# Down projection: accumulating transfers issued four pairs ahead, token sums split before the sums that wait

## The chip, the cores and the metric

The kernel runs on one core of a Trainium2 chip. The metric is device time in microseconds (us) of one execution. The time before is the median of three runs. Engines: TensorE (PE, with its weight loads PEld), VectorE (DVE), ScalarE (ACT), GpSimd (POOL), SyncE (SP); 16 DMA engines move data between HBM and the on-chip buffers.

## What is computed

One layer of a hybrid encoder on 256 tokens of width 2048, in float32: a half-step SwiGLU feed-forward network (FFN), a mixer (a gated recurrence beside windowed attention), and a second FFN, each between RMS norms. The change touches the two FFNs' last matrix product alone, the down projection:

```python
def swiglu(x, w_gate_up, w_down):
    gate, up = jnp.split(x @ w_gate_up, 2, axis=-1)
    return (jax.nn.silu(gate) * up) @ w_down

ff = swiglu(rms_norm(x, pre_norm_ffn1[layer]), w_ffn1_gate_up[layer], w_ffn1_down[layer])
x = x + 0.5 * rms_norm(ff, post_norm_ffn1[layer])
```

`w_down` has 5632 rows and 2048 columns in float32 (46 MB in each of the two FFNs), and is read from HBM once.

## The kernel before

**Products.** A float32 operand is split into a high part `h` (a cast on ScalarE, L176) and a low part `l` (the source minus `h`, on VectorE, L177). A product is three matmuls: high x high, high x low, low x high (`three`, L435; the matmul is L441). The 256 tokens are two halves of 128 (m), the columns of a run two halves of 512 (n).

**Pairs, runs and steps.** The 5632 rows are 22 pairs of 256 (two blocks of 128, k). The projection is done in two runs of 1024 columns, each over all 22 pairs in the order of `orders` (L1197). A step is one pair of one run: steps 0 to 21 are run 0, 22 to 43 run 1; the last two pairs of run 1 (20, 21) are held for `finish` (L705). The silu-gated activations of a pair lie in a tile `ht`. Eight of the `ht` tiles (pairs 0 to 7) are put away to HBM earlier and fetched into four buffers (`fetch`, L1063, at the steps of `fetch_at`).

**Two kinds of pair.** A plain pair (odd numbers, 20 and 21) is 2 x 2 x 2 products, 24 matmuls, and its weights are split in two halves of 128x1024 (`split_half`, L168). A pair by sums (even numbers 0 to 18, `MIXED`) uses a scheme with seven products in place of eight, 21 matmuls (`products`, L485). It needs sums of weight blocks and sums of token blocks (the token sums). With b11, b12, b21, b22 the four 128x512 blocks of the raw weights, its steps are, in `splits` (L1238): split b11 alone (`ha`, `la`); form two block sums (L1255, one VectorE operation on 128x1024), or let a DMA do it; split the lower half; b22 = b11 + b22 (L1259); b21 = b22 + b21 (L1260); split the upper half; split the lower half again (the last half). The token sums, formed once when the activations were made, are split into `sp` (`left_sums`, L635). The order of use on TensorE: three matmuls with `ha`/`la`; three with the lower half; from the seventh on `sp` is needed; from the tenth the upper half; from the sixteenth the last half.

**Accumulating transfers.** For the pairs in `added` (L1202) the two block sums of L1255 are made by a DMA: `prepare(i)` (L1228) splits b11 into `ha`, `la` and then issues, on POOL's queue, a transfer of 512 KB that adds b12 and b22, read again from HBM, onto the first two blocks of the raw buffer (L1232). POOL waits for `la`, since the transfer overwrites b11. L1259 is the first operation on VectorE that reads the result.

**Order.** The loop at L1318 is under a schedule written by hand: what is written first is issued first on each engine. Iteration i does: first part of `splits(i + 1)`; `prepare(i + 3)`; fetches; second part of `splits(i + 1)`; the matmuls of step i; the last part of `splits(i + 1)`. In a pair by sums the parts end after L1260, after the upper half, and after the last half and `sp`.

**Loads.** Five raw buffers of 1 MB are in turn: three that last the whole kernel and two in the pool `hb`. When the last half of a pair has been split, its buffer takes the next load in the order `coming` (`load_down`, L1211), on SP's queue. `in_order` (L1204) sorts the steps, with those in `added` 2.5 places early. Loads from step 39 on (`NU + 17`) go to the lasting buffers only, since the pool `hb` is closed at step 40.

**Kept sums.** Run 0's splits of the token sums of pairs 0 and 2 (`near`) and 16 and 18 (`keep`) are kept for run 1; the others are split again. The unsplit sums of 16 and 18 are made during run 0 (`sums_again`, L1026, tile `su`).

**Fold.** After a run's last pair by sums, its four extra banks `p` are added to the four result banks `c` (`fold`, L513): in run 0 within step 20, in run 1 at step 41, ahead of that step's matmuls. After run 0 `second_run` (L698) drains the four banks `c` with ScalarE (squares) and VectorE (gains).

Of the kernel before, what the change touches and what calls it, by code (L numbers as in the profile page):

```python
# [12 lines left out]
F32R = mybir.dt.float32r  # L13
# [7 lines left out]
P = 128  # L21
# [16 lines left out]
def hymba_layer_kernel(  # L38
# [37 lines left out]
    def nm(s):  # L76
        uid[0] += 1
        return f"{s}_{uid[0]}"
# [89 lines left out]
    def split_half(raw, i, hp=hip, lp=lop):  # L168
        part = raw[:, i * 1024 : (i + 1) * 1024]
        h = hp.tile([P, 1024], F32R, tag="h", name=nm("h"))  # L170
        l = lp.tile([P, 1024], F32R, tag="l", name=nm("l"))
        split_act(h, l, part)
        return h, l

    def split_act(hi, lo, src):
        nc.scalar.copy(hi, src)  # L176
        nc.vector.tensor_tensor(lo, src, hi.bitcast(F32), ALU.subtract)  # L177
# [11 lines left out]
    far = {}  # L189
# [142 lines left out]
    class LeadN:  # L332


        def __init__(self, w, c0, slot):
            self.w, self.c0, self.slot = w, c0, slot
# [259 lines left out]
    class Pairs(Blocks):  # L596
# [2 lines left out]


        HELD = 2

        def __init__(self, w, orders, tiles, sums, room, gain_src, keep=(), near=()):

# [45 lines left out]

        def one_block(self):
            return (
                far["pool"].tile([P, 512], F32R, tag=t, name=nm(t)) for t in ("ha", "la")
            )

        def half_gain(self, pool):
# [48 lines left out]
        def finish(self, mul, post, new_x=None, gain=None, lead=None):  # L705
# [4 lines left out]
            self.post = post  # L710
            self.work(n_order - self.HELD)
            held = []
            for u in order[n_order - self.HELD :]:
                held.append((u, *split_load(self.source(u), hp=post, lp=post)))
# [150 lines left out]
    NU = DFF // 256  # L865
# [5 lines left out]
    MIXED = range(0, 20, 2)  # L871
# [133 lines left out]
    def ffn(gated, w_dn, post_gain, again, gain=None, lead=None, aside=None):  # L1005

        with ExitStack() as st:
            work = st.enter_context(tc.tile_pool(name=nm("wk"), bufs=1, reuse_waits="tile"))
# [5 lines left out]
            hts, sums, away = [], {}, {}  # L1014
# [165 lines left out]
            def pair_ahead(g, u):  # L1180
# [16 lines left out]
            orders = [  # L1197
                [9, 11, 8, 13, 10, 15, 12, 1, 0, 3, 14, 5, 16, 17, 2, 7, 4, 19, 6, 18, 20, 21],

                [7, 2, 9, 4, 11, 6, 13, 8, 10, 15, 0, 5, 12, 3, 14, 1, 16, 18, 17, 19, 20, 21],  # L1200
            ]
            added = {0: (12, 0, 14, 16, 2, 4, 6), 1: (2, 4, 6, 8, 0, 12, 14, 16)}  # L1202
            steps = [(r, u) for r in range(2) for u in orders[r]][: 2 * NU - Pairs.HELD]
            in_order = sorted(  # L1204
                (i - 2.5 if u in added[r] else i, i) for i, (r, u) in enumerate(steps)
            )
            coming = [i for _, i in in_order]
            raws, firsts, got = {}, {}, {}
            rows = None

            def load_down(raw):  # L1211
                if coming and (coming[0] < NU + 17 or any(raw is one for one in gated.lasting)):
                    i = coming.pop(0)
                    r, u = steps[i]
                    dst = raw.rearrange("p (k c) -> p k c", k=2)
                    nc.sync.dma_start(dst, Pairs.part(w_dn, u, r))
                    raws[i] = raw
# [10 lines left out]
            def prepare(i):  # L1228
                if i < len(steps) and steps[i][1] in added[steps[i][0]]:
                    r, u = steps[i]  # L1230
                    first_block(i)
                    nc.gpsimd.dma_start(  # L1232
                        raws[i][:, 0:1024].rearrange("p (k c) -> p k c", k=2),
                        Pairs.part(w_dn, u, r)[:, :, 512:1024],
                        accum_op=ALU.add,
                    )

            def splits(i):  # L1238
                if i >= len(steps):
                    return  # L1240
                r, u = steps[i]
                raw = raws[i]
                parts = got[i] = []
                b11, b12, b21, b22 = blocks(raw)
                if u not in MIXED:
                    parts.append(split_half(raw, 0))
                    yield
                    parts.append(split_half(raw, 1))
                    load_down(raw)
                    yield  # L1250
                    return
                four = raw.rearrange("p (i c) -> p i c", i=4)
                if i not in firsts:
                    first_block(i)
                    nc.vector.tensor_tensor(  # L1255
                        four[:, 0:2], four[:, 0::3], four[:, 1:2].to_broadcast([P, 2, 512]), ALU.add
                    )
                parts.append(split_half(raw, 1))
                nc.vector.tensor_tensor(b22, b11, b22, ALU.add)  # L1259
                nc.vector.tensor_tensor(b21, b22, b21, ALU.add)  # L1260
                yield
                parts.append(split_half(raw, 0))
                yield
                parts.append(split_half(raw, 1))
                load_down(raw)
                rows.left_sums_ahead(u)
                yield

            def products(i, among=None):
# [11 lines left out]
            with tc.manual_schedule():  # L1281
                gated.prepare(1, MIXED_IN[0])
                some(gated.splits(1, 0), 2)
                for g in range(1, NG):
                    first_pairs(g, waiting)
                    for u in range(2, last - 1):
                        pair_ahead(g, u)
                    some(gated.splits(g, last), 2)
                    if g < NG - 1:
                        gated.prepare(g + 1, MIXED_IN[0])  # L1290
                    for one in gated.take(g, last - 1):
                        one()
                    boundary(g, gated.splits(g + 1, 0) if g < NG - 1 else splits(0))
                    waiting = units(gated.c, rest)
                    some(waiting, 2)
                room_cm.__exit__(None, None, None)
                close_far()
                back_cm = tc.tile_pool(name=nm("hb"), bufs=AWAY // 2, reuse_waits="tile")
                back = back_cm.__enter__()
                fetch_at = {2: (1, 0), 3: (3,), 5: (5,), 9: (2,), 10: (7,), 11: (4,), 13: (6,)}  # L1300
                fetch_at.update({26: (0, 5), 28: (3,), 30: (1,)})
                again_at = {8: 16, 14: 18}
                for u in MIXED[8:]:
                    sums[u] = None
                rows = Pairs(w_dn, orders, hts, sums, work, post_gain, keep=MIXED[8:], near=MIXED[:2])
                some(waiting, 2)
                ahead = splits(1)
                some(ahead, 2)
                products(0)
                for _ in range(2):  # L1310
                    load_down(back.tile([P, 2048], F32, tag="raw", name=nm("raw"), bufs=2))
                some(waiting, 1)
                ahead = splits(2)
                some(ahead, 2)
                some(waiting, 1)
                some(ahead, 1)
                products(1)
                for i in range(2, len(steps)):  # L1318
                    if i == NU + 18:
                        back_cm.__exit__(None, None, None)  # L1320
                        early_cm.__exit__(None, None, None)
                        post = rows.post = st.enter_context(post_pool())
                    ahead = splits(i + 1)
                    next(ahead, None)
                    prepare(i + 3)
                    for u in fetch_at.get(i, ()):
                        fetch(u)
                    next(ahead, None)
                    products(i)
                    for _ in ahead:  # L1330
                        pass
                    if i in again_at:
                        sums[again_at[i]] = sums_again(again_at[i])
                    if i == 8:
                        rows.half_gain(far["pool"])
                    if i == NU - 1:
                        rows.second_run()
# [8 lines left out]
    gated = Gated(w_ffn1_gate_up[0], two_banks())  # L1346
    xt = new_xt()
    gated.see(xt)
    with tc.manual_schedule():
# [9 lines left out]
        raw = rawp.tile([P, 2048], F32, tag="raw", name=nm("raw"))  # L1359
# [121 lines left out]
    with ExitStack() as s2:  # L1481
# [111 lines left out]
        keep = [mid.tile([P, 2, 2, P], F32, tag=f"keep{j}", name=f"keep{j}") for j in range(2)]  # L1593
# [286 lines left out]
        orders = [[0, 1, 4, 6, 5, 7, 2, 3], [0, 4, 1, 5, 6, 7, 2, 3]]  # L1880
        rows = Pairs(w_mix_out[0], orders, yt, ysums, yroom, post_norm_mix)
# [3 lines left out]
        gated = Gated(w_ffn2_gate_up[0], two_banks())  # L1885
# [80 lines left out]
```

## Time and profile before

| | us |
|---|---|
| median of 3 runs | 1848.81 |
| lowest and highest | 1846.79, 1853.28 |
| the profiled execution | 1848.27 |
| its span, first to last instruction | 1846.4 |
| mean granted TensorE clock | 0.997 |

In that execution the down projection's steps 0 to 41 run from 477.62 to 705.20 us in the first FFN and from 1602.10 to 1826.69 us in the second; the text calls the two FFNs layers where it counts per layer. The rows below come from the page of the profile (busy time of engines, groups of instructions), from its views of busy time by stretch, of waits, of DMA issues, and from the timeline. A group's row has: line, engine, operation, out<-in, shape, count | busy us, mean ns of one | idle us of the engine just before them and who ended it. `L177 DVE` is an instruction of line 177 on VectorE; `pa` and `pb` are the result banks.

### The profile page before, as it was taken

Reading aid. Unit: us, or ns where it says so; the run is one execution under the profiler, and the core shown is the slowest. Engines: PE = TensorE matmul, PEld = TensorE weight load, DVE = VectorE, ACT = ScalarE, POOL = GpSimd, SP = SyncE. Lnnn points to the kernel's source line nnn. Section 1 sums busy time; section 2 is a strip of 40 time slices with the busy share of each in tenths; the row PEclk is TensorE's granted clock in tenths of the full one; section 3 lists DMA queues with packets and bytes.
Section 4 is the critical chain, followed back from the end, with each engine's and each line's share of the span. In section 5 each row is a group of like instructions: output and inputs, shape, how many; then the busy total and the mean of one; then the engine's idle time right before and its main releaser. Section 6 shows DMA issues by size and latency. Waiting matters only on the chain.

```text
span 1846.4 us, 23441 instructions
## 1 busy us (share of the span) xinstructions
PE 1819.5 (99%) x8438; PEld 1504.8 (82%) x8438; DVE 1601.5 (87%) x2041; ACT 1128.7 (61%) x1492; POOL 150.7 (8%) x145
## 2 busy tenths in 40 slices
PE   9999999999999999999999999999999999999997
PEld 6888888888877787888888888788888888878876
DVE  7999999999889888477687798899999999989886
ACT  6566666655556556476587557556666665556563
POOL 1011111111010100000000000011111111010110
PEclk9999999999999999999999999999999999999999
DMA  8789999989697885656554456789989989698874
GB/s 299 228 237 282 277 279 253 257 251 253 242 310 242 248 275 187 207 176 179 171 171 148 162 210 247 227 236 271 283 265 275 250 250 252 214 310 283 267 241 166
DMA packets 209332, 442.35 MB, mean 240 GB/s; under 512 B 11592, under 2 KB 46496, under 8 KB 208448
## 3 DMA queue, kind: packets, MB, share of 16 engines
q1 hardware_dynamic: 180032, 385.14, 59.5%
q0 software_dynamic: 29184, 55.72, 17.8%
q8 instruction: 66, 1.08, 0.2%
q14 instruction: 50, 0.41, 0.1%
HBM read 428.21 MB, written 12.60 MB: 239 GB/s over the span
## 4 chain that ended last, share of the span: by engine, by line
PE 71%; DMA 9%; issue 9%; DVE 8%; ACT 3%; POOL 1%; SPq 0%; DVEq 0%; ACTq 0%; POOLq 0%
PE pa L441 29%; PE pb L441 25%; DMA raw<-in_w_ffn_down_dram 6%; PE pa L309 5%; DVE l L177 3%; PE pa L314 3%; DMA raw<-in_w_ffn_gate_up_dram 2%; PE pa L364 2%; PE pa L363 2%; PE pa L362 2%; ACT h L176 1%; DVE raw L1259 1%; DVE la L177 1%; POOL raw L1232 0%; PE pa L1098 0%
## 5 line engine op out<-in xcount | busy, mean ns | idle before, releaser
L176 ACT CAST h<-raw 128x1024 fp32r<-128x1024 f32 (+1 forms) x861 | 851.1, 1013 | 484.6 <-PE pb L441 154.7
L177 DVE TENSOR_TENSOR l<-raw,h 128x1024 fp32r<-128x1024 f32 (+1 forms) x861 | 981.2, 1171 | 122.1 <-ACT h L176 90.2
L441 PE MATMUL pa<-h,xt 128*128 128x512 f32 x1104 | 387.6, 392 | 0.1
L441 PE MATMUL pb<-h,xt 128*128 128x512 f32 x952 | 340.7, 392 | 0.4 <-DVE pb L1150 0.4
L441 PEld LDWEIGHTS pa<-h,xt 128*128 128x128 f32 x1104 | 207.2, 188 | 44.2 <-DVE xt L232 0.6
L441 PE MATMUL pa<-l,xt 128*128 128x512 f32 x552 | 215.5, 390 | 0.0
L441 PEld LDWEIGHTS pb<-h,xt 128*128 128x128 f32 x952 | 178.7, 188 | 43.8 <-DVE pb L1157 3.9
L441 PE MATMUL pb<-l,xt 128*128 128x512 f32 x476 | 185.6, 390 | 0.0
L441 PE MATMUL pa<-h,ht 128*128 128x512 f32 x464 | 163.2, 390 | 2.6 <-DVE pa L535 2.6
L441 PE MATMUL pb<-h,ht 128*128 128x512 f32 x464 | 163.2, 390 | 0.0
L934 POOL DMA_DIRECT2D raw<-in_w_ffn_gate_up_dram x76 | 92.0, 1211 | 737.7 <-DVE l L177 654.6
L309 PE MATMUL pa<-xt,h 128*128 128x512 f32 x512 | 124.4, 393 | 0.2 <-ACT h L176 0.2
L441 PEld LDWEIGHTS pa<-l,xt 128*128 128x128 f32 x552 | 103.8, 188 | 20.6 <-DVE l L177 0.5
L309 PEld LDWEIGHTS pa<-xt,h 128*128 128x128 f32 x512 | 93.8, 188 | 18.6 <-ACT h L176 0.6
L441 PE MATMUL pa<-h,xs 128*128 128x512 f32 x304 | 108.9, 389 | 0.0
L441 PE MATMUL pb<-h,xs 128*128 128x512 f32 x304 | 106.0, 389 | 0.0
L441 PEld LDWEIGHTS pa<-h,ht 128*128 128x128 f32 x464 | 87.1, 188 | 21.6 <-issue 2.3
L441 PEld LDWEIGHTS pb<-l,xt 128*128 128x128 f32 x476 | 89.4, 188 | 17.0
L441 PEld LDWEIGHTS pb<-h,ht 128*128 128x128 f32 x464 | 87.4, 188 | 18.2
L441 PE MATMUL pb<-l,ht 128*128 128x512 f32 x232 | 90.5, 390 | 0.0
L441 PE MATMUL pa<-l,ht 128*128 128x512 f32 x232 | 90.3, 389 | 0.0
L441 PE MATMUL pa<-h,sp 128*128 128x512 f32 x176 | 63.8, 404 | 10.1 <-DVE sp L177 6.7
(287 smaller groups left out, 2529.7 us busy)
## 6 DMA issues: line engine op xcount, KB each, us to landing
raw<-in_w_ffn_gate_up_dram SPq DMA_DIRECT2D x350, 512.0 KB, 5.9
raw<-in_w_ffn_down_dram SPq DMA_DIRECT2D x88, 1024.0 KB, 7.5
raw<-in_w_mix_in_dram SPq DMA_DIRECT2D x52, 1024.0 KB, 4.9
raw<-in_w_ffn_gate_up_dram POOLq DMA_DIRECT2D x76, 512.0 KB, 8.7
raw<-in_w_mix_out_dram SPq DMA_DIRECT2D x16, 1024.0 KB, 5.1
raw<-in_w_ffn_down_dram POOLq DMA_DIRECT2D x30, 512.0 KB, 6.3
ht<-away SPq DMA_DIRECT2D x24, 512.0 KB, 9.4
away<-ht SPq DMA_DIRECT2D x16, 512.0 KB, 7.0
```

The costliest lines, as they stand in the source:

```text
L176: nc.scalar.copy(hi, src)
L177: nc.vector.tensor_tensor(lo, src, hi.bitcast(F32), ALU.subtract)
L309: nc.tensor.matmul(slot[f], weights(hs, kk, f), xcol(xt, k), start=(k == 0), stop=(k == KT - 1))
L314: nc.tensor.matmul(slot[f][:, 0:T], weights(ls, kk, f), xcol(xt, kh * 8 + kk, 0), start=False, stop=False,)
L362: nc.tensor.matmul(dst, xh, h[:, o : o + n], start=(k == 0), stop=False)
L363: nc.tensor.matmul(dst, xh, l[:, o : o + n], start=False, stop=False)
L364: nc.tensor.matmul(dst, xl, h[:, o : o + n], start=False, stop=(k == KT - 1))
L441: nc.tensor.matmul(self.bank(at), lhs, rhs, start=(n == 1), stop=n in (ends, self.of[at]), skip_group_check=n > ends,)
L934: nc.gpsimd.dma_start(raw[:, 0:1024].rearrange("p (k c) -> p k c", k=2), self.source(u, g)[:, :, 1], accum_op=ALU.add,)
L1259: nc.vector.tensor_tensor(b22, b11, b22, ALU.add)
```

## The change

It issues the accumulating transfers one step earlier (`prepare(i + 4)`) and moves the loads of their pairs one place ahead in the order of loads (3.5 places instead of 2.5); gives the FFNs' `ha` and `la` three buffers each instead of two; splits the token sums right after a pair's first half, ahead of L1259, instead of at the end; adds pair 18 to the accumulating ones in run 0, and 10 and 18 in place of 8 in run 1 (8 and 9 instead of 7 and 8); gives run 1 another order, which begins with pair 2; no longer keeps the splits of 16 and 18; lets loads of steps 39 and 40 go to any buffer; and shifts some fetches by a step.

```diff
--- before.py
+++ after.py
@@ -599,6 +599,7 @@
 
 
         HELD = 2
+        firsts = 2
 
         def __init__(self, w, orders, tiles, sums, room, gain_src, keep=(), near=()):
 
@@ -650,7 +651,8 @@
 
         def one_block(self):
             return (
-                far["pool"].tile([P, 512], F32R, tag=t, name=nm(t)) for t in ("ha", "la")
+                far["pool"].tile([P, 512], F32R, tag=t, name=nm(t), bufs=self.firsts)
+                for t in ("ha", "la")
             )
 
         def half_gain(self, pool):
@@ -1197,19 +1199,19 @@
             orders = [
                 [9, 11, 8, 13, 10, 15, 12, 1, 0, 3, 14, 5, 16, 17, 2, 7, 4, 19, 6, 18, 20, 21],
 
-                [7, 2, 9, 4, 11, 6, 13, 8, 10, 15, 0, 5, 12, 3, 14, 1, 16, 18, 17, 19, 20, 21],
+                [2, 7, 4, 9, 6, 11, 8, 13, 10, 12, 15, 0, 5, 14, 3, 16, 1, 18, 17, 19, 20, 21],
             ]
-            added = {0: (12, 0, 14, 16, 2, 4, 6), 1: (2, 4, 6, 8, 0, 12, 14, 16)}
+            added = {0: (12, 0, 14, 16, 2, 4, 6, 18), 1: (2, 4, 6, 10, 12, 0, 14, 16, 18)}
             steps = [(r, u) for r in range(2) for u in orders[r]][: 2 * NU - Pairs.HELD]
             in_order = sorted(
-                (i - 2.5 if u in added[r] else i, i) for i, (r, u) in enumerate(steps)
+                (i - 3.5 if u in added[r] else i, i) for i, (r, u) in enumerate(steps)
             )
             coming = [i for _, i in in_order]
             raws, firsts, got = {}, {}, {}
             rows = None
 
             def load_down(raw):
-                if coming and (coming[0] < NU + 17 or any(raw is one for one in gated.lasting)):
+                if coming and (coming[0] < NU + 19 or any(raw is one for one in gated.lasting)):
                     i = coming.pop(0)
                     r, u = steps[i]
                     dst = raw.rearrange("p (k c) -> p k c", k=2)
@@ -1256,6 +1258,7 @@
                         four[:, 0:2], four[:, 0::3], four[:, 1:2].to_broadcast([P, 2, 512]), ALU.add
                     )
                 parts.append(split_half(raw, 1))
+                rows.left_sums_ahead(u)
                 nc.vector.tensor_tensor(b22, b11, b22, ALU.add)
                 nc.vector.tensor_tensor(b21, b22, b21, ALU.add)
                 yield
@@ -1263,7 +1266,6 @@
                 yield
                 parts.append(split_half(raw, 1))
                 load_down(raw)
-                rows.left_sums_ahead(u)
                 yield
 
             def products(i, among=None):
@@ -1297,12 +1299,13 @@
                 close_far()
                 back_cm = tc.tile_pool(name=nm("hb"), bufs=AWAY // 2, reuse_waits="tile")
                 back = back_cm.__enter__()
-                fetch_at = {2: (1, 0), 3: (3,), 5: (5,), 9: (2,), 10: (7,), 11: (4,), 13: (6,)}
-                fetch_at.update({26: (0, 5), 28: (3,), 30: (1,)})
+                fetch_at = {2: (1,), 3: (0,), 5: (3,), 6: (5,), 9: (2,), 10: (7,), 11: (4,), 13: (6,)}
+                fetch_at.update({25: (0,), 26: (5,), 28: (3,), 29: (1,)})
                 again_at = {8: 16, 14: 18}
                 for u in MIXED[8:]:
                     sums[u] = None
-                rows = Pairs(w_dn, orders, hts, sums, work, post_gain, keep=MIXED[8:], near=MIXED[:2])
+                rows = Pairs(w_dn, orders, hts, sums, work, post_gain, near=MIXED[:2])
+                rows.firsts = 3
                 some(waiting, 2)
                 ahead = splits(1)
                 some(ahead, 2)
@@ -1322,7 +1325,7 @@
                         post = rows.post = st.enter_context(post_pool())
                     ahead = splits(i + 1)
                     next(ahead, None)
-                    prepare(i + 3)
+                    prepare(i + 4)
                     for u in fetch_at.get(i, ()):
                         fetch(u)
                     next(ahead, None)
```

## Prediction

> **What bounds the kernel now.** The page first: TensorE is hardly ever idle, so only a place where it waits, or runs slowly, can give time back.
>
> ```profile
> span 1846.4 us, 23441 instructions
> PE 1819.5 (99%) x8438; PEld 1504.8 (82%) x8438; DVE 1601.5 (87%) x2041; ACT 1128.7 (61%) x1492; POOL 150.7 (8%) x145
> ```
>
> A busy PE is not one at its peak, so the second view is the busy time by stretch, cut at the steps of the two down projections (columns: PE, PEld, DVE, ACT, POOL busy with counts, granted clock, DMA share, GB/s; the two rows with one count are of L441's matmuls alone).
>
> ```profile
> 477.62:596.08 118.46, 115.09 (x508) 93.89 (x506) 105.42 (x124) 68.52 (x84) 9.71 (x8) 1.00 0.88 289
> 596.08:652.40 56.32, 53.45 (x226) 43.18 (x225) 47.66 (x52) 33.24 (x39) 6.05 (x5) 0.97 0.82 262
> 1602.10:1718.47 116.37, 114.94 (x507) 93.92 (x506) 105.18 (x124) 68.62 (x84) 9.68 (x8) 1.00 0.90 294
> 1718.47:1774.39 55.92, 53.52 (x227) 43.16 (x225) 47.57 (x52) 33.23 (x39) 6.05 (x5) 0.97 0.83 265
> 1640.78:1676.82 36.04, 36.04 (x161) 29.85 (x160) 31.48 (x39) 22.09 (x25) 4.84 (x4) 1.00 1.01 338
> 692.52:705.20 12.68, 11.15 (x49) 1.00 0.72 257
> 1814.51:1826.69 12.18, 11.16 (x50) 1.00 0.23 88
> ```
>
> The fifth row is steps 7 to 13 of the second FFN: by the code 3 x 21 + 4 x 24 = 159 matmuls (two of the 161 only reach in) without a wait, so one takes 36.04 / 159 = 0.2267 us when nothing is late. A run has 10 x 21 + 12 x 24 = 498 of them, 112.9 us. Rows 1 and 3 (run 0) also hold eight transposes, which take 0.79 us:
>
> ```profile
> 1607.54 0.27 PE L1098 MATMUL pa<-ident,z 128*128 128x128 f32 x1
> 1608.33 0.48 PE L441 MATMUL pa<-h,ht 128*128 128x512 f32 x1
> ```
>
> Run 0 thus loses 118.46 - 112.9 - 0.8 = 4.8 us in the first FFN and 116.37 - 113.7 = 2.7 us in the second. Rows 2 and 4 are steps 22 to 31, 5 x 21 + 5 x 24 = 225 matmuls, 51.0 us: 5.3 and 4.9 us are lost. Together **17.7 us**. Part of it is clock: 0.97 in those rows, 0.03 x 56 = 1.7 us each.
>
> Third, who is waited for (the waits of 477 to 690, then of 1600 to 1812; total, times, longest):
>
> ```profile
> PEld pa L441 <- DVE sp L177: 5.9, 5, 1.5
> PEld pa L441 <- ACT sp L176: 3.3, 2, 1.9
> DVE raw L1259 <- DMA raw<-in_w_ffn_down_dram: 15.2, 9, 4.9
> ...
> PEld pa L441 <- DVE sp L177: 5.0, 5, 1.5
> PEld pa L441 <- ACT sp L176: 1.7, 2, 1.2
> DVE raw L1259 <- DMA raw<-in_w_ffn_down_dram: 15.6, 10, 4.1
> ```
>
> TensorE waits only for `sp`, the split token sums, and VectorE, which makes them, sits 15 us per layer before L1259, for the accumulating transfer to land. The timeline of VectorE at step 6 shows the one making the other:
>
> ```profile
> 1626.12 2.55 DVE L177 TENSOR_TENSOR l<-raw,h 128x1024 fp32r<-128x1024 f32 x2
> 1632.75 0.69 DVE L1259 TENSOR_TENSOR raw<-raw 128x512 f32<-128x512 f32 x1 [4.08 <-DMA raw<-in_w_ffn_down_dram]
> 1633.48 0.69 DVE L1260 TENSOR_TENSOR raw<-raw 128x512 f32<-128x512 f32 x1
> 1634.09 0.68 DVE L177 TENSOR_TENSOR la<-raw,ha 128x512 fp32r<-128x512 f32 x1
> 1634.69 2.35 DVE L177 TENSOR_TENSOR l<-raw,h 128x1024 fp32r<-128x1024 f32 x2
> 1636.96 0.68 DVE L177 TENSOR_TENSOR sp<-sums,sp 128x512 fp32r<-128x512 f32 x1
> ...
> 1762.46 0.19 PEld L441 LDWEIGHTS pa<-h,sp 128*128 128x128 f32 x1 [1.20 <-ACT sp L176]
> 1764.26 0.30 PEld L441 LDWEIGHTS pa<-h,sp 128*128 128x128 f32 x2 [1.50 <-DVE sp L177]
> ```
>
> 4.08 us idle, and `sp` is the last of six operations behind it. `la` of step 8 is queued there as well, so the next accumulating transfer is issued late too. The last two rows are step 30 (10 right behind 8), the costliest place.
>
> **The change part by part.** Unit prices, from the groups of 1600 to 1718 and from the instructions on the tile `su` (last row):
>
> ```profile
> L177 DVE TENSOR_TENSOR l<-raw,h 128x1024 fp32r<-128x1024 f32 x56 | 66.4, 1219 | 1.0 <-ACT h L176 0.8
> L177 DVE TENSOR_TENSOR la<-raw,ha 128x512 fp32r<-128x512 f32 x11 | 7.5, 686 | 0.0
> L1260 DVE TENSOR_TENSOR raw<-raw 128x512 f32<-128x512 f32 x10 | 6.9, 692 | 0.3
> L1255 DVE TENSOR_TENSOR raw<-raw 128x1024 f32<-128x1024 f32 x3 | 3.7, 1225 | 0.1
> L176 ACT CAST sp<-su x4: 614/614/617, 540.8 to 1702.4; 128x512 fp32r<-128x512 f32 x4
> L177 DVE TENSOR_TENSOR sp<-su,sp x4: 683/684/687, 542.5 to 1703.7; 128x512 fp32r<-128x512 f32 x4
> ```
>
> *Four pairs ahead.* An accumulating transfer is issued one step earlier, 4.8 or 5.4 us (21 or 24 matmuls). The longest wait before L1259 was 4.9, so nearly all of the 15 us go. What issuing costs (cast `ha`, subtract `la` 0.69, the transfer on POOL's queue) is only moved; a third `ha`/`la` buffer keeps it from waiting for the buffer of the pair in work.
>
> *Does VectorE keep up without its waits?* A pair by sums costs it 3 x 1.22 + 0.69 + 2 x 0.69 + 0.68 = 6.4 us, a plain one 2.4: 8.8 per couple against 45 x 0.2267 = 10.2 us of TensorE. It gains 1.4 us per couple and can stay ahead. Of the neighbours, 18 in run 0 and 10, 12 in run 1 (steps 30, 31) are now all accumulated: 2 x 6.4 = 12.8 us for 42 matmuls, 9.5; the 3.3 missing are made up in the plain steps 29 and 32, 3.0 each. Before, 8 and 10 cost 6.4 + 6.4 + 1.2 (L1255; `la` is paid either way) = 14.0.
>
> *Sums split ahead.* `sp` is needed after 6 of the 21 matmuls, the last half after 15: what is last now may be 9 x 0.2267 = 2.0 us later than `sp` could. Late next is that last half. The 1.20 + 1.50 of step 30 would not fit under 2.0, so this part alone leaves some 0.7 there. ScalarE's cast of `sp` is put where it waits for L1260 anyway.
>
> *16 and 18 not kept.* Run 1 splits their sums again, 2 x 0.68 on VectorE and 2 x 0.61 on ScalarE per layer; one L1255 (1.23) goes from each run, since one more pair accumulates in each. Nothing on the path: the freed 15 us cover it; uncovered it is 2 x (2 x 0.68 - 1.23) = 0.3 us.
>
> *Run 1 begins with 2.* Its first products go to banks that no drain of run 0 holds, and its sums are kept: at or below nothing, taken as 0. The fetches moved by one step find their buffers read (2 and 7 are now used at steps 22 and 23): 0.
>
> *Loads of plain pairs come later.* Five raw buffers are shared, and the loads for accumulating pairs move ahead, so a plain pair's load is issued when the pair three before it has been split, not four: two steps of lead, about one couple. Against it stand the landings (the window 1650 to 1700, medians; then the accumulating and later weight loads of the whole kernel, min/median/max):
>
> ```profile
> q1 hardware_dynamic: 3590, 13.72, 70.2%
> q0 software_dynamic: 1091, 2.10, 25.6%
> raw<-in_w_ffn_down_dram SPq DMA_DIRECT2D x9, 1024.0 KB, 8.2
> raw<-in_w_ffn_down_dram POOLq DMA_DIRECT2D x4, 512.0 KB, 7.7
> DMA to landing us min/median/max: 4.8/7.4/10.9
> ```
>
> 8.2 fits under 8.8 to 10.2, barely. And here the DMA engines are full (share 1.01 in the clean row). An accumulating transfer takes them 0.256 x 50 / 4 = 3.2 us, and one more of run 0 falls into this stretch. Bounds per layer: 0, if the idle DMA time around step 6 takes it up, to 3.2, if none does. The queue is full for most of run 0, so I take the middle, 1.6.
>
> The Trainium skill, DMA: Bandwidth & Descriptors, section Where 436 GB/s comes from, says that HBM to SBUF transfers are bound by HBM at about 358 GB/s per core. By that, the clean row's 338 GB/s leaves 6%, and I would estimate 0.52 MB / 358 GB/s = 1.5 us per layer in place of 1.6, 0.2 us off the sum; no row here shows whether 358 is the limit.
>
> *The clock.* 0.97 stands only where the two waits of step 30 lie; with them it goes, and its 1.7 us is inside the 17.7. If it were set by something else, 3.4 us would stay. The Trainium skill, TensorE: Matmul & The Clock Gate, section What's actually happening, has the clock halve after an idle window of about 3.4 us; 1.20 + 1.50 is under that, so by that rule the loss would not be theirs and the sum 3.4 us higher. The row sides with the waits.
>
> *The fold at step 41.* 12.68 - 48 x 0.2267 = 1.8 and 1.3 us are lost there:
>
> ```profile
> 1815.58 0.69 DVE L529 TENSOR_TENSOR y<-pb,y 128x512 f32<-128x512 f32 x1
> 1816.22 1.23 DVE L177 TENSOR_TENSOR l<-raw,h 128x1024 fp32r<-128x1024 f32 x1
> ```
>
> Halves of the last two pairs stand between the adds. Taken as unchanged; bounds -3.1 (both waits go) and +4.9 (two more halves of 1.22 ahead of the fold, in each layer).
>
> **The sum**, on the profiled execution's 1848.27 us (median of the runs 1848.81, 0.5 higher): 1848.3 - 17.7 + 2 x 1.6 = **1833.8 us**. All bounds at their best 1848.3 - 17.7 - 3.1 = 1827.5; at their worst 1848.3 - 17.7 + 6.4 + 4.9 + 3.4 = 1845.3.
>
> **Rivals.**
> - *The wait only moves at the neighbours.* If VectorE does not enter steps 30 and 31 ahead, TensorE waits for the last half there. For it: two pairs by sums still stand together, 3.3 us short. Against: they are 1.2 us cheaper and a 2.4 us step stands before them. Only run 0's 4.8 + 2.7 is gained: 1848.3 - 7.5 = 1840.8.
> - *Slower: plain loads late in run 0.* Where loads queue behind the earlier accumulating transfers, every couple takes as long as a plain load's landing. It decides once landings pass 10.2 us; over the six couples of steps 2 to 13 in both layers the 17.7 is eaten at 10.2 + 17.7 / 12 = 11.7. At 12.5 (10.9, the longest above, plus half a transfer of 3.2) it is 1848.3 - 17.7 + 12 x 2.3 = 1858.2. For it: share 1.01. Against: TensorE ran at full pace in that very row, so what was asked was delivered.
> - *It doesn't do what it says.* If VectorE is held by the DMA's pace, the transfers are issued earlier and land no earlier: run 0 unchanged, run 1 better by a little, about 1845.
>
> **How the numbers follow.** 0.3% (5.5 us) is about what can be told from no change. Forecast 0.68, wait moved 0.13, no effect 0.08, slower 0.11. Faster is the first two less a little, 0.80; same 0.09; slower 0.11. The forecast's own range, by its bounds, is 1827 to 1845, and the second case lies in it; it leaves 0.19 out.
>
> **What would show it.** Right: the waits before L1259 fall from 15 us per layer to under 4; no `sp` row among PE's waits; the clock at 1.00 in steps 22 to 31; both runs within 2 us of count x 0.2267. Wrong: PE waiting for `l` or `h` of a raw block at step 31, plain casts waiting for weight loads in run 0, landings over 10 us, or a longer fold.

## The result, and the profile after

The changed kernel takes 1834.23 us (median of 4 runs, 1832.72 to 1835.36) against 1848.78 us before (4 runs, 1846.79 to 1853.28): ratio 0.9917, 95% interval 0.9898 to 0.9937. The prediction was 1833.8. In the profiled executions the span went from 1846.4 to 1830.9 us, 15.5 less. The page after, its span, the engines' busy time, and the chain of waits by engine:

```profile
span 1830.9 us, 23436 instructions
PE 1812.4 (99%) x8438; PEld 1503.5 (82%) x8438; DVE 1599.2 (87%) x2041; ACT 1130.9 (62%) x1496; POOL 155.5 (8%) x149
PE 89%; DVE 4%; ACT 3%; DMA 2%; issue 2%; POOL 0%; SPq 0%; DVEq 0%; ACTq 0%; POOLq 0%
```

The engines have about as much to do as before: VectorE is busy for 1599.2 us in place of 1601.5, and TensorE does the same 8438 instructions. TensorE stands for 89% of the chain that ended last (71% before). The time came from waits. The busy time by stretch, cut at the same steps as before the change (columns as in the prediction):

```profile
477.08:590.86 113.78, 113.78 (x508) 94.33 (x506) 105.09 (x124) 68.91 (x82) 12.12 (x10) 1.00 0.96 310
590.86:641.34 50.48, 50.48 (x224) 41.62 (x222) 47.90 (x54) 35.42 (x45) 6.04 (x5) 1.00 0.93 292
682.14:695.22 13.08, 11.16 (x49) 8.93 (x48) 12.56 (x15) 5.79 (x7) 0.00 (x0) 1.00 0.58 197
1593.15:1706.92 113.77, 113.77 (x507) 94.33 (x506) 105.33 (x124) 68.99 (x82) 12.10 (x10) 1.00 0.95 310
1706.92:1757.40 50.48, 50.48 (x223) 41.60 (x222) 47.99 (x54) 35.09 (x45) 6.04 (x5) 1.00 0.92 288
1798.20:1811.27 13.07, 11.15 (x49) 8.94 (x48) 10.30 (x13) 3.81 (x5) 0.00 (x0) 1.00 0.01 1
```

Run 0 takes 113.78 us, and 498 x 0.2267 + 0.8 = 113.7: nothing is lost any more, where 4.8 and 2.7 us were. Steps 22 to 31 are now 6 x 21 + 4 x 24 = 222 matmuls, 50.3 us; 0.15 is lost in place of 5.3 and 4.9. The clock there is 1.00. One place got worse: steps 40 and 41, 48 matmuls or 10.88 us of work, lose 13.08 - 10.88 = 2.2 us per layer (1.8 and 1.3 before).

Who is waited for, after (477 to 690, VectorE then TensorE; then VectorE in 1590 to 1795, a window that ends before the fold of the second layer, whose wait is 1.9 us too):

```profile
DVE l L177 <- ACT h L176: 17.4, 20, 1.5
PEld pa L441 <- DVE y L692: 0.3, 1, 0.3
PE pa L441 <- DVE pa L535: 1.9, 1, 1.9
...
DVE l L177 <- ACT h L176: 16.3, 21, 1.4
```

There is no `sp` row, and no row of VectorE before L1262 (the line that was L1259). What idle time VectorE has left is behind ScalarE's casts, which themselves wait, in the first layer, 35.6 us for TensorE to free `h` buffers, 28.9 us for VectorE's own sum at L1263 and 5.0 us for weight loads. TensorE waits for none of it: VectorE is ahead. The 1.9 us is the fold.

The DMA side did not get easier. Issues with their median landing: 1600 to 1650 after the change (two rows), the accumulating ones of 1600 to 1650 before it, and of 1640 to 1690 after it, the part of the layer that stood at 1650 to 1700 before; last, all weight transfers of the kernel after:

```profile
raw<-in_w_ffn_down_dram SPq DMA_DIRECT2D x10, 1024.0 KB, 8.6
raw<-in_w_ffn_down_dram POOLq DMA_DIRECT2D x5, 512.0 KB, 11.0
...
raw<-in_w_ffn_down_dram POOLq DMA_DIRECT2D x3, 512.0 KB, 6.3
...
raw<-in_w_ffn_down_dram POOLq DMA_DIRECT2D x5, 512.0 KB, 9.0
...
DMA to landing us min/median/max: 4.8/8.3/12.3
```

An accumulating transfer lands after 11.0 us in the median early in the layer, where it was 6.3, and after 9.0 in the next part, where it was 7.7, and VectorE waits for none of them. So the transfers did not become faster; they were taken off the path. There are also more of them: two more per layer, each of which reads half of a pair's weights a second time, 2.1 MB in all (444.45 MB moved in place of 442.35).

### The profile page after: what moved, and what is told of

Its sections match the earlier page's. It is cut to its first block, busy times and chain, and to the rows that moved or that the text cites. A ratio compares the mean times of both kernels' runs of the same rounds, so it can differ in the third digit from the quotient of the medians.

```text
span 1830.9 us, 23436 instructions
## 1 busy us (share of the span) xinstructions
PE 1812.4 (99%) x8438; PEld 1503.5 (82%) x8438; DVE 1599.2 (87%) x2041; ACT 1130.9 (62%) x1496; POOL 155.5 (8%) x149
## 2 busy tenths in 40 slices
DMA packets 210420, 444.45 MB, mean 243 GB/s; under 512 B 11656, under 2 KB 46560, under 8 KB 209536
## 4 chain that ended last, share of the span: by engine, by line
PE 89%; DVE 4%; ACT 3%; DMA 2%; issue 2%; POOL 0%; SPq 0%; DVEq 0%; ACTq 0%; POOLq 0%
PE pa L441 39%; PE pb L441 33%; PE pa L309 5%; PE pa L314 3%; PE pa L364 2%; PE pa L363 2%; PE pa L362 2%; DVE l L177 2%; DMA raw<-in_w_ffn_gate_up_dram 2%; ACT h L176 1%; PE pa L1100 1%; PE pb L1100 1%; PE pb L1690 0%; PE pb L1664 0%; PE pb L1768 0%
## 5 line engine op out<-in xcount | busy, mean ns | idle before, releaser
L1234 POOL DMA_DIRECT2D raw<-in_w_ffn_down_dram x34 | 41.2, 1211 | 366.2 <-DVE la L177 345.9
```

The costliest lines, as they stand in the source:

```text
L1234: nc.gpsimd.dma_start(raws[i][:, 0:1024].rearrange("p (k c) -> p k c", k=2), Pairs.part(w_dn, u, r)[:, :, 512:1024], accum_op=ALU.add,)
```

## The experiments

All compare the time from a layer's first down matmul to the first of the held pairs, since chips and executions differ by some us elsewhere (the kernel before took 1852.18 in the first set of runs, 1850.15, median of 11, in the second, 1845.03 in the third). 948 matmuls and the transposes are 948 x 0.2267 + 0.8 = 215.7 us; what is over is lost.

| kernel | time, us | layer 1, us | layer 2, us | lost in both |
|---|---|---|---|---|
| before | 1848.78 | 227.58 | 224.59 | 20.8 |
| changed | 1834.23 | 218.15 | 218.12 | 4.9 |
| before, sums early | 1857.47 | 229.63 | 231.67 | 29.9 |
| before, four ahead | 1836.69 | 221.80 | 218.46 | 8.9 |
| changed, sums late | 1834.08 | 219.78 | 218.19 | 6.6 |
| changed, three ahead | 1846.27 | 223.21 | 226.84 | 18.7 |
| changed, fold first | 1827.81 | 215.96 | 215.94 | 0.5 |
| changed, again | 1834.63 | 219.71 | 218.14 | 6.5 |
| changed, loads later | 1886.58 | 245.74 | 243.96 | 58.3 |
| before, prepared ahead of the wait | 1834.26 | 219.29 | 218.82 | 6.7 |
| the same, sums early | 1829.13 | 216.28 | 216.22 | 1.1 |
| changed, three ahead, prepared ahead of the wait | 1833.34 | 218.44 | 218.48 | 5.5 |

The times are medians of several runs for before, changed, fold first and again; the others ran once. The layers are those of one profiled execution each.

**1. The parts alone.** Four kernels. The sums early, on the kernel before:

```diff
                 parts.append(split_half(raw, 1))
+                rows.left_sums_ahead(u)
                 nc.vector.tensor_tensor(b22, b11, b22, ALU.add)
...
                 load_down(raw)
-                rows.left_sums_ahead(u)
                 yield
```

> The kernel before with one edit: the token sums are split right after a pair's first half. Theory (VectorE idles before L1259 until the accumulating transfer lands, and sums split early hide up to 2.0 us of it): the waits before L1259 stay at about 15 us per layer, TensorE's waits for sp go, some 0.7 us per layer stays as a wait for the last half at step 30; lost in the two runs 1 to 4 us in place of 17.7, time 1833 to 1838. Rival (only the earlier issue counts, and without it VectorE is as late with the last half as it was with sp): half or more of the 17.7 stays, time 1840 to 1847.

Neither held. It is slower than before, by 9.1 us of lost time (5.3 us against the 1852.18 of the kernel before in the same set, one run each). Its waits (1600 to 1812; L1260 is the b22 sum there), and VectorE at step 38:

```profile
PEld pa L441 <- DVE l L177: 5.6, 8, 1.6
DVE raw L1260 <- DMA raw<-in_w_ffn_down_dram: 25.6, 12, 6.2
...
1805.95 0.69 DVE L1260 TENSOR_TENSOR raw<-raw 128x512 f32<-128x512 f32 x1 [6.15 <-DMA raw<-in_w_ffn_down_dram]
```

TensorE no longer waits for `sp` but for the last half, `l`, and VectorE waits longer for the transfers, 25.6 us in place of 15.6. What TensorE used to lose at `sp` in the middle is now lost at the end, where no later step can make it up: 1804.78 to 1835.84 (steps 38 to 41, 90 matmuls, 20.4 us of work) takes 31.06 us, 10.7 too many where the same steps lost 1.3 before. By the granted clock of 0.89, some 3.4 us of it is clock.

```profile
1804.78:1835.84 31.06, 24.71 (x91) 18.48 (x90) 24.41 (x27) 13.94 (x15) 0.00 (x0) 0.89 0.34 122
```

Another part has to do with other transfers. The buffer that takes `X` again (2 MB in two loads, L1463) holds unsplit token sums until then, so sums that are split earlier free it earlier. In the kernel before (first fence) these loads are issued after the run's last accumulating transfer, here (second fence) ahead of it:

```profile
1791.66 1.20 POOL L1232 DMA_DIRECT2D raw<-in_w_ffn_down_dram  x1 [9.00 <-DVE la L177]
1794.15 1.13 SPq L1463 DMA_DIRECT2D X<-kept  x2
```

```profile
1791.62 0.81 SPq L1463 DMA_DIRECT2D X<-kept  x2
1794.54 1.20 POOL L1232 DMA_DIRECT2D raw<-in_w_ffn_down_dram  x1 [7.61 <-DVE la L177]
```

That transfer landed after 6.2 us before and after 11.3 us here; the 6.15 us at L1260 above is the wait for it. The first layer has the same order and 6.0 against 11.3 us. So about 5 us per layer, as much as the whole of the 9.1, may come from the order of these loads. No run separates the two; what is shown is that the sums split early alone gain nothing.

The earlier issue alone, on the kernel before (the lines that give `ha` and `la` a third buffer, as in the change, are left out here and in the next diff):

```diff
-                (i - 2.5 if u in added[r] else i, i) for i, (r, u) in enumerate(steps)
+                (i - 3.5 if u in added[r] else i, i) for i, (r, u) in enumerate(steps)
-                rows = Pairs(..., keep=MIXED[8:], near=MIXED[:2])
+                rows = Pairs(..., near=MIXED[:2])
+                rows.firsts = 3
-                    prepare(i + 3)
+                    prepare(i + 4)
```

> The kernel before with the earlier issue alone: transfers four pairs ahead, their loads 3.5 places early, three buffers for ha and la; 16 and 18 are not kept, which makes the room. Orders, accumulating pairs and the place of the token sums as before. Theory: the waits before L1259 fall from 15 to under 4 us per layer; steps 6 and 14 lose nothing; at step 30 (8 and 10 as neighbours, 14.0 us of VectorE for 9.5 of TensorE) a wait of 1 to 2 us per layer may stay: time 1832 to 1837. Rival (sums split early do it all): TensorE still waits for sp, over 8 of the 17.7 us stay, time 1839 or more.

As the theory had it, 1836.69: the waits before b22 (L1261 here) are a single one of 0.5 us in the first layer, and TensorE keeps small waits for `sp`, 2.4 and 1.0 us.

```profile
DVE raw L1261 <- DMA raw<-in_w_ffn_down_dram: 0.5, 1, 0.5
PEld pa L441 <- DVE sp L177: 2.4, 4, 1.0
```

Then the same two parts taken back from the changed kernel. First the diff of the sums, reversed:

> The changed kernel with the token sums split last again. Theory: VectorE is ahead without it, lost in the two runs under 2 us, time 1833 to 1836. Rival (sums split early do it all): waits for sp come back, at the neighbours 10 and 12 above all, 8 us or more lost, time 1842 or more.

1834.08, and the 1.6 us by which its first layer is longer than the changed kernel's is clock (0.55 over 690.40 to 692.80 us, behind the fold's wait; last section); the two runs lose nothing else but the fold. In the changed kernel it makes no difference where the sums are split. Then `prepare(i + 3)` and 2.5 places in the changed kernel:

> The changed kernel with transfers three pairs ahead and loads 2.5 places early again. Theory: VectorE waits before b22 = b11 + b22 again, 10 to 15 us per layer; the sums that are split early hide most: 1 to 4 us lost in the two runs, time 1834 to 1838. Rival (only the earlier issue counts): 8 us or more lost, time 1842 or more.

1846.27: the rival's number. The waits before b22 are back (1600 to 1812), and TensorE waits for the last half, and for the drain after run 0 (`y`, L692):

```profile
DVE raw L1262 <- DMA raw<-in_w_ffn_down_dram: 20.9, 11, 5.9
PEld pa L441 <- DVE l L177: 4.6, 4, 1.9
PEld pa L441 <- DVE y L692: 2.0, 1, 2.0
```

So 12 of the 14.6 us hang on the earlier issue, and splitting the sums early hides nothing by itself. That is against my own theory of the 2.0 us of cover, and leaves the question what it is about the fourth pair.

**2. Lead, or place.** In the kernel before, `prepare(i + 3)` stands in the same iteration as the splits of pair i + 1, behind its b22 sum. With every second pair accumulating, a pair's `la`, and so its transfer, is queued on VectorE behind the wait for the transfer before it. Each is issued when the last has landed: 2 us of VectorE and a landing of 6 to 10 us against the 10.2 that a couple takes TensorE. `prepare(i + 4)` falls, for all but a few pairs, in the iteration of a plain pair, where nothing is waited for. To tell this from the fourth pair, three pairs ahead were kept and two lines exchanged (the transfer still goes out earlier, by the wait and some 2 us of VectorE):

```diff
                     ahead = splits(i + 1)
+                    prepare(i + 3)
                     next(ahead, None)
-                    prepare(i + 3)
```

> The kernel before, still three pairs ahead with loads 2.5 places early and token sums split last, but the preparation is written ahead of the first part of the next pair's splits, so ha, la and the transfer no longer stand behind the wait for the transfer before (three buffers for ha and la, 16 and 18 not kept, for the room). Theory (it was the place behind L1259 that held the kernel: a transfer was only issued when the one before had landed, 2 us of VectorE plus a landing of 6 to 10 us per couple of pairs that takes TensorE 10.2): two transfers are in flight now, waits before L1259 fall under 6 us per layer, 10 us or more of the gain come without a fourth pair of lead, time 1834 to 1840. Rival (the lead in time is what counts, and this adds only some 3 us to it): more than 10 us per layer of waits stay, time 1841 to 1847.

1834.26 against 1850.15, all of the gain without the fourth pair. The third buffers and the unkept sums, which this run has too, are not the reason: the changed kernel with three pairs ahead has both and loses 18.7 us. Its waits in the second layer, and its issues beside those of the kernel before:

```profile
DVE raw L1261 <- DMA raw<-in_w_ffn_down_dram: 3.7, 4, 2.7
1620.43 1.22 POOL L1234 DMA_DIRECT2D raw<-in_w_ffn_down_dram  x1 [9.15 <-DVE la L177]
1621.39 0.69 DVE L1261 TENSOR_TENSOR raw<-raw 128x512 f32<-128x512 f32 x1 [0.24 <-DMA raw<-in_w_ffn_down_dram]
```

```profile
1634.09 0.68 DVE L177 TENSOR_TENSOR la<-raw,ha 128x512 fp32r<-128x512 f32 x1
1635.19 1.22 POOL L1232 DMA_DIRECT2D raw<-in_w_ffn_down_dram  x1 [11.38 <-DVE la L177]
```

In the first fence the next transfer is issued at 1620.43, 1 us ahead of the wait for the one before, which ends at 1621.39. In the second, before the change, that wait ends at 1632.75 and the issue follows at 1635.19. The changed kernel with the same exchange:

> The changed kernel with transfers three pairs ahead and loads 2.5 places early, but prepared ahead of the first part of the next pair's splits. Theory (two transfers in flight is what counts, not the fourth pair): nothing lost in the runs but the fold's 2 us per layer, time 1831 to 1836, 10 us less than with three pairs ahead behind the wait (1846.27). Rival (the fourth pair counts): 1840 or more.

1833.34, 13 us under the same three pairs behind the wait (5.5 us lost in place of 18.7). And the sums early, on the run with the exchange:

> The run with the preparation ahead of the first part (three pairs ahead), and in addition the token sums split early. Theory (splitting the sums early did harm only where each transfer is issued behind the landing of the one before): the 1.1 to 1.6 us at step 30 go, the tail loses the fold's 2 us alone, time 1831 to 1835. Rival (early sums harm by themselves, since they delay b22 and the last half): losses of 1 us or more at steps 20 and 38 to 40 as in the run with the sums alone, time 1838 or more.

1829.13, under the range of either theory: nothing lost at step 30 (1.6 and 1.1 us in the run without), and 0.5 per layer in all. So with this order of pairs splitting the sums early is worth having once no transfer is issued behind another's landing, and gains nothing before that. The fold loses 0.4 here in place of 1.7, for which I had no reason beforehand; VectorE's timeline of the second layer has one half between the fold's adds ahead of L535, where the run without has two, and such halves are the matter of the next run.

**3. The fold.** Of the 4.9 us that the changed kernel loses, 4.4 lie in steps 40 and 41. VectorE there (second layer): of the five halves of 128x1024 shown, three belong to the held pairs, by comparison with the run below: the last of the three ahead of L529, and the two between the adds. All stand ahead of L535, the first add into a result bank.

```profile
1796.81 3.50 DVE L177 TENSOR_TENSOR l<-raw,h 128x1024 fp32r<-128x1024 f32 x3 [0.81 <-ACT h L176]
1800.23 0.69 DVE L529 TENSOR_TENSOR y<-pb,y 128x512 f32<-128x512 f32 x1
1800.83 1.22 DVE L177 TENSOR_TENSOR l<-raw,h 128x1024 fp32r<-128x1024 f32 x1
1801.96 0.68 DVE L522 TENSOR_TENSOR y<-pb,y 128x512 f32<-128x512 f32 x1
1802.56 1.22 DVE L177 TENSOR_TENSOR l<-raw,h 128x1024 fp32r<-128x1024 f32 x1
...
1804.89 0.69 DVE L535 TENSOR_TENSOR pa<-pa,y 128x512 f32<-128x512 f32 x1
```

```diff
-            add(c[1][1], c[1][1], y22, ALU.add)
+            self.fold_end = add(c[1][1], c[1][1], y22, ALU.add)
...
-                held.append((u, *split_load(self.source(u), hp=post, lp=post)))
+                raw = load(self.source(u))
+                with tc.issue_after(self.fold_end.ins):
+                    held.append((u, *split(raw, post, post)))
```

> The changed kernel with the split halves of the last two pairs of a run put behind the fold's adds on VectorE. Theory (the 2.1 us that each layer loses between steps 40 and 41 are the three halves of 1.22 us that stand ahead of the fold's first add into a result bank): under 0.5 us is lost there, the held halves are still ready before the held products; 3 to 4 us less in all, time 1830 to 1831. Rival (the fold waits for its own inputs, or the held halves come late instead): 0 to 1 us less, or the same 2 us lost at the held products.

> The changed kernel as it is, beside the one before on the same chip: 15 us less by both theories, ratio 0.992; it is there to compare the fold first with.

The fold first takes 1827.81 us (1827.63 to 1827.92), ratio 0.9877 (0.9858 to 0.9897), beside the changed kernel's 1834.63 (1832.28 to 1836.05), ratio 0.9913 (0.9898 to 0.9928): 6.8 us less, more than either theory had. The layers say why: 215.96 and 215.94 against 219.71 and 218.14. 2.2 us in each is the fold, 1.6 more in the first is the clock after the wait; some 0.9 lies outside the two stretches. After L529 the adds now follow each other, and the four held halves come behind them, still ready in time:

```profile
1796.98 0.68 DVE L529 TENSOR_TENSOR y<-pb,y 128x512 f32<-128x512 f32 x1
...
1799.63 0.69 DVE L535 TENSOR_TENSOR pa<-pa,y 128x512 f32<-128x512 f32 x1
...
1802.02 4.62 DVE L177 TENSOR_TENSOR l<-raw,h 128x1024 fp32r<-128x1024 f32 x4
```

This is the fastest version of the study.

**4. The slower case.** How near is the margin of the plain loads? 5.5 places instead of 3.5 in the order of loads of the changed kernel, which takes another pair of lead from the plain ones:

> The changed kernel with the loads of accumulating pairs 5.5 places early, which leaves a plain pair's load one pair of lead in place of two. Theory (the slower case of the prediction: a load that lands after its lead sets the pace): lead is about 6.4 us of VectorE's work, landings 8 to 10, so 0.5 to 2 us per couple of pairs are lost in most couples, ScalarE's casts of raw blocks wait for weight loads, time 1842 to 1870. Rival (there is far more room than the prediction saw): under 2 us more than the changed kernel.

1886.58, 52 us slower than the changed kernel and beyond the range. ScalarE's waits in the second layer, and the stretch:

```profile
ACT h L176 <- DMA raw<-in_w_ffn_down_dram: 32.3, 10, 7.5
1621.19:1865.15 243.96, 224.92 (x957) 181.27 (x956) 195.13 (x222) 128.91 (x156) 20.55 (x17) 0.97 0.80 252
```

Two pairs of lead cost nothing; one costs 26 to 28 us per layer, of which, by the clock of 0.97 over 244 us, some 7 are clock. The DMA engines are less full than in the changed kernel (0.80 against 0.87): it is lead, not throughput, that is missing.

## Why the prediction was right, point by point

- *What can be gained*, 17.7 us: right. 0.1 is lost in each run 0, and 0.15 in steps 22 to 31, so 17.2 came back.
- *Cause: waits before L1259 make `sp` late*: right, by the runs with three and four pairs ahead (18.7 and 4.9 lost). But the step "an accumulating transfer is issued one step earlier, 4.8 or 5.4 us" put it down to the longer lead. The exchange of two lines shows that the place behind the wait was what held the kernel; three pairs are enough. (More lead that still stands behind a wait was not run.) The prediction had read that `la` is queued there and that "the next accumulating transfer is issued late too", and drew nothing from it.
- *"Sums split ahead": 2.0 us of cover, some 0.7 left at step 30 if alone*: wrong. Alone it loses 9.1 us more, and in the changed kernel it is worth nothing. A wait that is hidden on TensorE did not shorten the chain of transfers that causes it; VectorE only fell back until the end. Nor had I counted what the earlier split sets off, the loads of `X` ahead of the last accumulating transfer.
- *VectorE keeps up, 8.8 against 10.2 us per couple, and the neighbours 10, 12 fit*: right. It idles 16 to 17 us per layer behind ScalarE's casts.
- *16 and 18 not kept, run 1 from pair 2, the fetches*: taken as 0, and run 1 loses 0.16 at its first step. With the old orders step 30 loses 0.4 us per layer in the run with four pairs ahead, 1.6 and 1.1 in the one prepared ahead of the wait, and nothing there once the sums are split early: what the new order is worth by itself was not run.
- *Plain loads and the full DMA engines, 2 x 1.6 us*: mis-sized, 0. The share rose from 0.88 to 0.96 in run 0 of the first layer, accumulating transfers landed after 11.0 us, and ScalarE waited 5.0 and 2.9 us for weight loads, all covered. That the slower case starts one pair of lead further on is shown by the run with later loads. The 358 GB/s that the prediction set beside this term is no limit here, and a row could have shown it: in the clean row of the kernel before, 1640.78 to 1676.82, cut into 40 slices of 0.9 us, eight slices in a row move 386 to 427 GB/s, and the mean of 338 comes from slices of 118 to 261 elsewhere in it.
- *The fold unchanged*: mis-sized. It lost 2.2 us per layer in place of 1.8 and 1.3, 1.3 more in all. I had bounds for it, and a reason (halves ahead of the adds), which the fold-first run bears out.
- *What would show it*: the waits before L1259 fell to none, and no `sp` row is left. But three signs that stood for a wrong forecast came as well, landings over 10 us, casts waiting for weight loads and a longer fold, and run 1 is 2.4 us over its count in place of 2. The first two show nothing as long as the loads keep their lead; the others are the fold.
- *The clock goes back to 1.00 with the waits of step 30*: right. In the kernel before it is 0.53 over 1765.20 to 1768.80 us, straight behind the two waits: 1.7 us, all that the 0.97 stands for.

The sum was worked out on the profiled execution, and there the time went from 1848.27 to 1832.72. So 1833.8 is 1.1 us too high: 3.2 us for the DMA engines were not lost, against 1.3 more at the fold, 0.5 in the two runs' remainders and some 0.4 outside the two stretches. The median, 1834.23, lies 1.5 us above that execution. That the sum comes within 0.4 us of it is luck.

## What to carry to other kernels

When an engine waits for a transfer, look at what is queued behind the wait: if the next transfer's preparation is there, transfers go one at a time, and each costs its preparation and its landing, here 2 us and 6 to 10 us. Write the preparation ahead of the wait before buying more buffers or lead. Hiding such a wait further down (the sums split early) did not shorten the chain here, and it let other loads go ahead of a transfer that was waited for; it paid only once the chain was gone. And split work for later must not be placed ahead of the adds that free a result bank for the next matmuls.

## What the runs showed of the hardware

The same wait has two prices. The changed kernel's fold wait in the first layer is 1.9 us in both profiled executions; after it the granted clock is 1.00 in one and about half in the other (windows of 2.4 us, the profiled execution of the result, then that of the second set of runs):

```profile
690.40:692.80 2.40, 2.40 (x12) 1.94 (x11) 2.40 (x4) 0.88 (x1) 0.00 (x0) 1.00 0.32 122
690.40:692.80 2.40, 2.40 (x6) 1.87 (x7) 2.40 (x4) 1.63 (x2) 0.00 (x0) 0.52 0.80 304
```

Six matmuls start in place of twelve, and the layer is 1.6 us longer (219.71 against 218.15). The Trainium skill, TensorE: Matmul & The Clock Gate, section What's actually happening, has the clock halve after an idle window of about 3.4 us, and says that the window runs freely; a wait of 1.9 us was enough here, so the length in that section is no safe limit, while the difference between two executions would fit its free-running window. Of the eight fold waits of 1.9 us in four profiled executions (the changed kernel twice, with the sums late, and with three pairs prepared ahead of the wait; two layers each), two were followed by the lower clock, the one above and that of the sums late. The version without the wait varies by 0.3 us between its runs, the one with it by 3.8.
